# Splitting the weights four units ahead instead of three, with three raw buffers instead of four, and z, one proj_a pair and some short steps moved

## The chip, the core and the metric

The program runs on one core of one Trainium2 chip. Five engines work side by side, each through its own list of instructions, in the order in which the list was built: PE (TensorE, matmuls and transposes), DVE (VectorE), ACT (ScalarE), POOL (GpSimd) and SP (SyncE). SP does nothing here but issue DMAs, POOL does it too. An engine that meets a semaphore that is not yet set stands still, and all that is behind in its list stands with it.

The metric is the device time of one execution in microseconds (us), from its first to its last instruction with what lies around it.

## What is computed

One layer of a decoder for 256 new tokens and 8 running sequences of one token each, 264 columns in all, model width 2048. Cut to what matters:

```python
h = rmsnorm(x, norm1_g)
q, f_logit, i_in, og, u_in, gate_a, gate_b = split(h @ w_in)        # w_in 2048 x 9216
o_h, S_new = hgrn2_recurrence(q, 1 - f, i_in, log(f), S0)           # 8 heads of 128, chunks of 16
o_a = rmsnorm_per_head(o_h) * silu(og)
y5, h_re, h_im = s5_scan(u_in, ...)                                 # 64 groups, 64 complex states each
z = gelu(y5)
zg = z @ w_s5_glu                                                   # 1024 x 2048
o_b = zg[:, :1024] * sigmoid(zg[:, 1024:])
merged = sigmoid(gate_a) * (o_a @ w_proj_a) + sigmoid(gate_b) * (o_b @ w_proj_b)
x = x + merged @ w_out
up = rmsnorm(x, norm2_g) @ w_ffn_up
x = x + (silu(up[:, :5632]) * up[:, 5632:]) @ w_ffn_down
y = rmsnorm(x, final_norm_g)
```

The outputs are y for all tokens and the new recurrent states.

## The kernel before

**Each product is made of three.** Every number is split into a high half that a matmul of the fast fp32r form takes exactly, and the rest: hi = round(w), lo = w - hi. A product is then hi·hi + lo·hi + hi·lo, three matmuls of 128 x 128 weights against 264 columns. The activations (h, oa, z, ob, m, x2g, ff) are split once when they are made, by `X.split`. The weights are split on the way: a **unit** of weights is four chunks of 128 rows by 256 columns, 512 KB; SP loads it into a `raw` buffer, ACT copies it to `hi` (line 151), DVE subtracts to `lo` (line 124). PE then runs 24 matmuls on a unit (4 chunks x 2 column halves x 3). I count the units from 0 in the order of use and write hi(n), lo(n) and L(n) for the high half, the low half and the load of unit n. Units 0 to 3 have two chunks and 12 matmuls.

**The buffers.** `NRAW = 4` raw buffers and `NSPL = 3` pairs of halves. In `gemm` each unit i first calls `load_to(i + NRAW + NSPL - 1)` and `split_to(i + NSPL)`: hi and lo of unit i + 2 are put into the lists of ACT and DVE just ahead of PE's unit i, into the halves that unit i - 1 has just left. L(n) goes into the raw buffer of unit n - 4 and waits on SP until lo(n - 4) has read it.

**The order.** The lists are written out by hand: `gemm` emits the matmuls of a half unit and then calls `advance`, which lets side tasks (generators: `s5_task`, `front_task`, `back_task`, `sample_task`, `z_task`, and evacuations of finished accumulators) put their next instructions behind them. A small model of the clocks of the engines (`clk`, `run`) decides how many steps a task may make; `yield 1` waits until the modelled results are there, `yield 0` only offers a pause. `run_until` forces steps until a condition holds. Nothing of this runs on the chip; what is on the chip is the resulting order.

**The stages.** Start: x is loaded and transposed, its norm is made, and `first_pairs` runs the first two column blocks (u0, u1; units 0 to 9) while `h_task` still makes h, chunk by chunk: DVE t = x·rs (`scaled`), ACT h_hi, DVE h_lo. Its loop gives the two units of a chunk group each a share of the next group's chunks, and `split_to(i + 2)` stands between them. Then the other blocks of w_in that feed HGRN2, S5 and gate b (`TURN`), with the recurrences as side tasks; their small matmuls and transposes stand between the large ones on PE. Then gate a and proj_a in turns (`pa_pair`, p = 0 to 7); `s5_task` ends about here (y of eight tiles, nt = 0 to 7, in place in `u_de`). `z_task` waits until all eight are there ("y") and makes z tile by tile: two GELU, z_hi, z_lo. Then the GLU product on z (four pairs, `glu_evac` makes ob), proj_b on ob (`pb_evac` makes m), w_out on m (`out_evac`), and the feed-forward part in two halves. The norm behind w_out is one matmul on the sum of squares `sqa` (`norm2_evac`).

The transposition of `pn` (parameters of S5), line 164 on PE, opens `s5_task`; DVE copies the last of it (`pn <- ld`, line 139) right before. gn holds the gains of the norms; `lb_evac` transposes it as the first evacuation behind the first pairs.

Of the kernel before, what the change touches and what calls it, by code (L numbers as in the profile page):

```python
# [9 lines left out]
F32 = mybir.dt.float32  # L10
# [20 lines left out]
NRAW = 4  # L31
NSPL = 3
# [33 lines left out]
def hybrid_step(ctx: ExitStack, tc: tile.TileContext, x_prompt, x_sample, state_hgrn, state_s5_re,  # L66
# [159 lines left out]
    for p in range(8):  # L226
        wlist(win, KD, [5120 + UN * q for q in ((0, 1) if p == 0 else (p + 1,) if p < 7 else ())])
        wlist(w_proj_a[0], 8, [UN * p])
    for q in range(4):
        wlist(w_s5_glu[0], 8, [1024 + UN * q, UN * q])  # L230
# [264 lines left out]
    gn = const.tile([64, P], F32, name="gn")  # L495
# [24 lines left out]
    load_to(4)  # L520
# [42 lines left out]
    tp(pg[:, 0, 0:16], gn1, ident[:16, :16])  # L563
    mm(pg[:, 0, 64:65], tok, ss[:, 5:6], True, True)
# [6 lines left out]
    vcopy(gvec[:, 0:16], pg[:, 0, 0:16])  # L571
    ts(vv[:, 2:3], pg[:, 0, 64:65], 1.0 / D, EPS, MUL, ADD)
# [16 lines left out]
    def h_task():  # L589
        t = {}  # L590

        def scaled(c):
            t[c] = spt.tile([P, NT], F32, tag="t", name="t")
            tt(t[c], xt[:, c], rsb if c else pg[:, 1, 0:NT], MUL)

        scaled(0)
        split_to(1)
        act(rsb, pg[:, 1, 0:NT])
        for c in range(KD):
            u = halves(t.pop(c))  # L600
            hi, lo = lying(h.hi[:, c]), lying(h.lo[:, c])
            act(hi, u, scale=gvec[:, c:c + 1])
            if c + 1 < KD:
                scaled(c + 1)
            stt(lo, u, gvec[:, c:c + 1], hi.bitcast(F32), MUL, SUB)
            h.upto(c + 1, clk["v"])
            if c in (2, 4):
                leave(c + 10, px[c // 2 + 1], act)
            yield
# [9 lines left out]
    def lb_evac():  # L619
        yield 1  # L620
        pg, = banks(1)
        tp(pg.t[:, :64], gn, ident[:64, :64])
        yield 1
        vcopy(gvec[:, 16:80], pg.t[:, :64])
        pg.done()
# [124 lines left out]
    def s5_task():  # L750
# [266 lines left out]
        u_done.add("y")  # L1017
# [12 lines left out]
        fo = small([32, 2, P], "fo")  # L1030
        fo2 = h0n
        act(flat(fo), po.t[0:32, 0:256])
# [21 lines left out]
    cmask = hp1.tile([P, 2, P], F32, name="cmask")  # L1054
    G.memset(cmask, 1.0)
    G.affine_select(out=cmask, in_=cmask, compare_op=ALU.is_ge, fill=0.0, base=0, pattern=[[0, 2], [1, P]],
                    channel_multiplier=-1)
    for a in range(2):
        cj = cmask[:, a].rearrange("p (j t) -> p j t", t=16)
        G.affine_select(out=cj, in_=cj, compare_op=ALU.is_ge, fill=0.0, base=0, pattern=[[-16, 8], [0, 16]],  # L1060
                        channel_multiplier=1)
# [75 lines left out]
    def front_task(p):  # L1137
# [98 lines left out]
        for j in range(2):  # L1236
            sv = flat(sc[:, 2 * j:2 * j + 2])
            act(sv, pas[j].t[:, 0:2 * P])
            yield 1
            where(sv, flat(cmask).bitcast(I32), pas[j].t[:, 2 * P:4 * P])  # L1240
            pas[j].done()
# [125 lines left out]
    def gb_evac(p):  # L1367
        def f(acc):
            sg = hp2.tile([P, 2, NT], F32, tag="sgb", name="sgb")
            act(sg, acc, AF.Sigmoid)  # L1370
            gdma(sgb_d[p], sg)
        return f
# [49 lines left out]
    def z_task():  # L1422
        while "y" not in u_done:
            yield 1
        for n in range(8):
            zt = mg2.tile([P, NT], F32, tag="zt", name="zt")
# [9 lines left out]
    for p in range(8):  # L1436
        pa_pair(p)
# [21 lines left out]
    for p in range(4):  # L1459
        sg = mg2.tile([P, 2, NT], F32, tag="sga", name="sga")  # L1460
        gemm(z, 8, sig_evac(sg))
        gemm(z, 8, glu_evac(p, sg))
    mgd = X(xa.tile([P, KD, NT], F32R, tag="xh", name="m_hi"), xa.tile([P, KD, NT], F32R, tag="xl", name="m_lo"))

    def pb_evac(p, sg):
        def f(acc):
            tt(sg, acc, sg, MUL)
            yield 1
# [51 lines left out]
    def norm2_evac():  # L1520
        yield 2
# [147 lines left out]
```

## Time and profile before

| | us |
|---|---|
| three runs before | 1465.81, 1466.18, 1466.27 (median 1466.18) |
| the profiled execution, whole | 1465.0 |
| its span, first to last instruction | 1463.3 |
| PE busy in the span | 1435.1 (98%) |
| DVE busy | 946.5 (65%) |
| ACT busy | 782.4 (53%) |

The matmuls of PE are pipelined: one of 264 columns is shown with 0.28 us, and the next begins 0.11 us after it. So "busy" says only that something was in the pipe, and an idle time that is shown begins when the modelled end of the last one is over. The views that name a wait give idle time only. DVE and ACT are shown with the times of their instructions, which overlap the next by a tenth of a microsecond.

### The profile page before, as it was taken

How to read it: one execution, taken by the hardware profiler on the slowest of the kernel's cores; microseconds unless marked ns; L12 is line 12 of the kernel's file. 1: busy time of each engine (PE TensorE's matmuls, PEld its weight loads, DVE VectorE, ACT ScalarE, POOL GpSimd, SP SyncE). 2: the span in 40 equal slices, each digit the busy share in tenths (PEclk: the TensorE clock that was granted, in tenths of full speed). 3: DMA queues.
4: the chain of work that ended last, by engine and by line, in shares of the span. 5: the costliest groups of instructions: out<-in, count | busy, mean ns of one | idle time of the engine just before them, and what ended most of it. 6: DMA issues, size and time to landing. Idle time of an engine off the chain costs nothing.

```text
span 1463.3 us, 31638 instructions
## 1 busy us (share of the span) xinstructions
PE 1435.1 (98%) x13298; PEld 1417.0 (97%) x13298; DVE 946.5 (65%) x1438; ACT 782.4 (53%) x1109; POOL 94.1 (6%) x170
## 2 busy tenths in 40 slices
PE   8999999999999999999999999999999999999996
PEld 7999999999999999999999999999999999999996
DVE  6588877777688875676665555554545555565553
ACT  6646667676756565445554444443434444445553
POOL 2401010112111010000000000000000000000000
PEclk9999999999999999999999999999999999999998
DMA  7867666677555447666656666655566666665553
GB/s 252 242 197 245 201 200 216 196 215 249 184 156 168 160 146 246 202 220 193 197 188 192 200 191 200 191 191 196 194 202 194 198 193 200 192 199 189 183 188 109
DMA packets 269072, 288.07 MB, mean 197 GB/s; under 512 B 10473, under 2 KB 260729, under 8 KB 268921
## 3 DMA queue, kind: packets, MB, share of 16 engines
q1 hardware_dynamic: 260144, 262.31, 56.2%
q0 software_dynamic: 8512, 23.63, 5.4%
q8 instruction: 104, 1.70, 0.5%
q14 instruction: 40, 0.32, 0.1%
q10 hardware_dynamic: 272, 0.11, 0.0%
HBM read 273.29 MB, written 12.71 MB: 195 GB/s over the span
## 4 chain that ended last, share of the span: by engine, by line
PE 55%; issue 2%; DVE 1%; DMA 0%; ACT 0%; POOL 0%; DVEq 0%; POOLq 0%
PE acc L380 18%; PE acc L379 18%; PE acc L378 18%; PE ps L164 0%; DMA sga<-sgb_d 0%; DVE lo L124 0%; PE ps L159 0%; POOL sga L168 0%; DVE rst L463 0%; DVE sga L124 0%; DVE yns L133 0%; DVE ynp L133 0%; ACT hi L151 0%; DVE rt L124 0%; DVE m_lo L124 0%
## 5 line engine op out<-in xcount | busy, mean ns | idle before, releaser
L124 DVE TENSOR_TENSOR lo<-raw,hi 128x1024 fp32r<-128x1024 f32 (+1 forms) x498 | 596.9, 1202 | 467.1 <-ACT hi L151 461.1
L151 ACT ACTIVATE hi<-raw 128x1024 fp32r<-128x1024 f32 (+1 forms) x498 | 514.8, 1038 | 585.7 <-PE acc L379 514.5
L378 PE MATMUL acc<-x2g_hi,hi 128*128 128x264 f32 x1408 | 388.8, 276 | 0.0
L380 PE MATMUL acc<-x2g_hi,lo 128*128 128x264 f32 x1408 | 388.7, 276 | 0.1
L379 PE MATMUL acc<-x2g_lo,hi 128*128 128x264 f32 x1408 | 388.6, 276 | 0.0
L378 PE MATMUL acc<-h_hi,hi 128*128 128x264 f32 x1088 | 305.7, 281 | 0.7 <-ACT hi L151 0.6
L380 PE MATMUL acc<-h_hi,lo 128*128 128x264 f32 x1088 | 301.3, 277 | 4.0 <-DVE lo L124 4.0
L379 PE MATMUL acc<-h_lo,hi 128*128 128x264 f32 x1088 | 300.3, 276 | 0.0
L380 PEld LDWEIGHTS acc<-x2g_hi,lo 128*128 128x128 f32 x1408 | 266.1, 189 | 0.3 <-DVE lo L124 0.3
L378 PEld LDWEIGHTS acc<-x2g_hi,hi 128*128 128x128 f32 x1408 | 266.1, 189 | 0.0
L379 PEld LDWEIGHTS acc<-x2g_lo,hi 128*128 128x128 f32 x1408 | 266.1, 189 | 0.0
L380 PEld LDWEIGHTS acc<-h_hi,lo 128*128 128x128 f32 x1088 | 205.6, 189 | 5.6 <-DVE lo L124 5.4
L378 PEld LDWEIGHTS acc<-h_hi,hi 128*128 128x128 f32 x1088 | 205.6, 189 | 2.9 <-ACT hi L151 1.1
L379 PEld LDWEIGHTS acc<-h_lo,hi 128*128 128x128 f32 x1088 | 205.7, 189 | 0.2
L378 PE MATMUL acc<-ff_hi,hi 128*128 128x264 f32 x704 | 195.0, 277 | 0.5 <-DVE x L124 0.5
L379 PE MATMUL acc<-ff_lo,hi 128*128 128x264 f32 x704 | 194.3, 276 | 0.0
L380 PE MATMUL acc<-ff_hi,lo 128*128 128x264 f32 x704 | 194.3, 276 | 0.0
L378 PEld LDWEIGHTS acc<-ff_hi,hi 128*128 128x128 f32 x704 | 133.1, 189 | 0.9 <-DVE x L124 0.7
L379 PEld LDWEIGHTS acc<-ff_lo,hi 128*128 128x128 f32 x704 | 133.1, 189 | 0.0
L380 PEld LDWEIGHTS acc<-ff_hi,lo 128*128 128x128 f32 x704 | 133.1, 189 | 0.0
L380 PE MATMUL acc<-m_hi,lo 128*128 128x264 f32 x256 | 70.8, 276 | 0.8 <-DVE lo L124 0.8
L378 PE MATMUL acc<-m_hi,hi 128*128 128x264 f32 x256 | 70.8, 276 | 0.1
(383 smaller groups left out, 1844.4 us busy)
## 6 DMA issues: line engine op xcount, KB each, us to landing
raw<-in_w_ffn_up_dram SPq DMA_DIRECT2D x176, 512.0 KB, 4.6
raw<-in_w_in_dram SPq DMA_DIRECT2D x142, 512.0 KB, 4.6
raw<-in_w_ffn_down_dram SPq DMA_DIRECT2D x80, 512.0 KB, 4.5
raw<-in_w_out_dram SPq DMA_DIRECT2D x32, 512.0 KB, 4.6
raw<-in_w_proj_a_dram SPq DMA_DIRECT2D x16, 512.0 KB, 3.4
raw<-in_w_s_glu_dram SPq DMA_DIRECT2D x16, 512.0 KB, 4.6
raw<-in_w_proj_b_dram SPq DMA_DIRECT2D x16, 512.0 KB, 4.5
s<-in_state_hgrn_dram POOLq DMA_DIRECT2D x8, 512.0 KB, 7.1
```

The costliest lines, as they stand in the source:

```text
L124: V.tensor_tensor(out, a, b, op=op)
L151: S.activation(out, a, f, **kw)
L378: PE.matmul(o, hi[:, q, s], xhi, start=(k0 + q == 0), stop=False)
L379: PE.matmul(o, hi[:, q, s], xlo, start=False, stop=False)
L380: PE.matmul(o, lo[:, q, s], xhi, start=False, stop=(k0 + q == k - 1))
```

## The change

- `NRAW` 3 instead of 4, `NSPL` 4 instead of 3. In `gemm`, hi and lo of unit i + 3 now stand where those of unit i + 2 stood; loads run as far ahead of PE as before (i + 6), through three raw buffers. At the start three loads instead of four are asked for.
- Room for the added halves: gn lies in a pool that ends with the start and is transposed there, with an ACT copy; `cmask` is kept once and broadcast; the S5 output tile `fo` uses `cx`; `sgb` has one buffer instead of two.
- `h_task` multiplies two chunks in one DVE instruction (`scaled`).
- `z_task` starts when tile 5 of S5 is there and takes tiles 6 and 7 as they come.
- The last proj_a pair runs behind the GLU product instead of ahead of it, and its weights are loaded in that order.
- `pb_evac` has one pause less; the matmul of `norm2_evac` is held until the model says that `sqa` is made.

```diff
-NRAW = 4
-NSPL = 3
+NRAW = 3
+NSPL = 4
...
     for p in range(8):
         wlist(win, KD, [5120 + UN * q for q in ((0, 1) if p == 0 else (p + 1,) if p < 7 else ())])
+        if p == 7:
+            for q in range(4):
+                wlist(w_s5_glu[0], 8, [1024 + UN * q, UN * q])
         wlist(w_proj_a[0], 8, [UN * p])
-    for q in range(4):
-        wlist(w_s5_glu[0], 8, [1024 + UN * q, UN * q])
...
-    gn = const.tile([64, P], F32, name="gn")
+    gn = sp.tile([64, P], F32, name="gn")
...
-    load_to(4)
+    load_to(NRAW)
...
     tp(pg[:, 0, 0:16], gn1, ident[:16, :16])
+    tp(pg[:, 0, 128:192], gn, ident[:64, :64])
...
     vcopy(gvec[:, 0:16], pg[:, 0, 0:16])
+    act(gvec[:, 16:80], pg[:, 0, 128:192])
...
         def scaled(c):
-            t[c] = spt.tile([P, NT], F32, tag="t", name="t")
-            tt(t[c], xt[:, c], rsb if c else pg[:, 1, 0:NT], MUL)
+            t[c] = spt.tile([P, 2, NT], F32, tag="t", name="t")
+            if c:
+                e = min(c % 2 + 1, KD - c)
+                tt(t[c][:, 0:e], xt[:, c:c + e], bc(rsb, 1, e), MUL)
+            else:
+                tt(t[0][:, 0], xt[:, 0], pg[:, 1, 0:NT], MUL)
...
-            if c + 1 < KD:
+            if c + 1 < KD and c % 2 == 0:
                 scaled(c + 1)
...
     def lb_evac():
-        yield 1
-        pg, = banks(1)
-        tp(pg.t[:, :64], gn, ident[:64, :64])
-        yield 1
-        vcopy(gvec[:, 16:80], pg.t[:, :64])
-        pg.done()
...
-        u_done.add("y")
+            u_done.add(("y", nt))
...
-        fo = small([32, 2, P], "fo")
+        fo = cx[0:32].rearrange("p r g n -> p r (g n)")
...
-    cmask = hp1.tile([P, 2, P], F32, name="cmask")
+    cmask = hp1.tile([P, P], F32, name="cmask")
...
-            sg = hp2.tile([P, 2, NT], F32, tag="sgb", name="sgb")
+            sg = hp1.tile([P, 2, NT], F32, tag="sgb", name="sgb")
...
     def z_task():
-        while "y" not in u_done:
-            yield 1
         for n in range(8):
+            while ("y", n if n > 5 else 5) not in u_done:
+                yield 1
...
-    for p in range(8):
+    for p in range(7):
         pa_pair(p)
     run_until(lambda: "s5" in u_done)
...
         gemm(z, 8, glu_evac(p, sg))
+    pa_pair(7)
...
             tt(sg, acc, sg, MUL)
-            yield 1
             tt(sg, sg, part[:, 2 * p:2 * p + 2], ADD)
...
     def norm2_evac():
-        yield 2
+        while not at_hand(sqa):
+            yield 1
```

Three places in the lists show what moves. The first is DVE at the end of the first pairs, before: `t` and `h_lo` make two chunks of h, `lo` is the low half of a unit's weights.

```order
L124 TENSOR_TENSOR lo<-raw,hi 128x1024
L124 TENSOR_TENSOR t<-xt,rsb 128x264
L128 SCALAR_TENSOR_TENSOR h_lo<-t,gvec,h_hi 128x264
L124 TENSOR_TENSOR t<-xt,rsb 128x264
L128 SCALAR_TENSOR_TENSOR h_lo<-t,gvec,h_hi 128x264
L124 TENSOR_TENSOR lo<-raw,hi 128x1024
```

And the same place after:

```order
L124 TENSOR_TENSOR lo<-raw,hi 128x1024
L124 TENSOR_TENSOR t<-xt,rsb 128x528
L128 SCALAR_TENSOR_TENSOR h_lo<-t,gvec,h_hi 128x264 x2
L124 TENSOR_TENSOR lo<-raw,hi 128x1024
L124 TENSOR_TENSOR t<-xt,rsb 128x264
L128 SCALAR_TENSOR_TENSOR h_lo<-t,gvec,h_hi 128x264 x2
```

Two products of 264 columns have become one of 528, which stands first behind the `lo`; only the last chunk still has its own.

The second place is DVE behind the first pairs, around the copy `pn`, for which PE's transposition waits. Before, from lo(11) on:

```order
L124 TENSOR_TENSOR lo<-raw,hi 128x1024 x2
L139 COPY gvec<-ps_712 128x64
L124 TENSOR_TENSOR lt<-gvec 128x8
L124 TENSOR_TENSOR lt<-gvec,lt 128x8 x2
L124 TENSOR_TENSOR lo<-raw,hi 128x1024 x2
L124 TENSOR_TENSOR lt<-lt 128x8
L633 RECIPROCAL lt<-lt 128x8
L124 TENSOR_TENSOR lbt<-lt 128x8
L135 TENSOR_SCALAR omlb<-lbt 128x8
L139 COPY pn<-ld_143 32x128
```

After, again from lo(11) on:

```order
L124 TENSOR_TENSOR lo<-raw,hi 128x1024 x3
L124 TENSOR_TENSOR lt<-gvec 128x8
L124 TENSOR_TENSOR lt<-gvec,lt 128x8 x2
L124 TENSOR_TENSOR lo<-raw,hi 128x1024 x2
L124 TENSOR_TENSOR lt<-lt 128x8
L634 RECIPROCAL lt<-lt 128x8
L124 TENSOR_TENSOR lbt<-lt 128x8
L135 TENSOR_SCALAR omlb<-lbt 128x8
L124 TENSOR_TENSOR lo<-raw,hi 128x1024
L139 COPY pn<-ld_143 32x128
```

`pn` stood behind lo(14) and now stands behind lo(16). On PE its transposition moves from the end of unit 12 (264 large matmuls behind the start) to the middle of unit 13 (276).

The third place is ACT at the end of S5: the last states (`hp`, `h`), two output copies, and z. Before:

```order
L151 ACTIVATE hp<-H_266 128x4
L151 ACTIVATE h_1118<-H_266 128x8x4
L151 ACTIVATE fo<-ps_7593 32x256
L151 ACTIVATE h0n<-ps_7594 128x512
L151 ACT_TABLE_LOAD
L151 ACTIVATE zt<-u_de 128x4x64
L151 ACTIVATE zt<-u_de 128x8
L151 ACTIVATE z_hi<-zt 128x264
L151 ACTIVATE hi<-raw 128x1024
L151 ACTIVATE zt<-u_de 128x4x64
L151 ACTIVATE zt<-u_de 128x8
L151 ACTIVATE z_hi<-zt 128x264
```

After:

```order
L151 ACTIVATE hp<-H_266 128x4
L151 ACTIVATE h_1159<-H_266 128x8x4
L151 ACTIVATE cx<-ps_7646 32x256
L151 ACTIVATE h0n<-ps_7647 128x512
L151 ACT_TABLE_LOAD
L151 ACTIVATE zt<-u_de 128x4x64
L151 ACTIVATE zt<-u_de 128x8
L151 ACTIVATE z_hi<-zt 128x264
L151 ACTIVATE hi<-raw 128x1024 x3
L151 ACT_TABLE_LOAD
L151 ACTIVATE sga<-acc 128x528
```

Before, these are the first of eight z tiles; after, seven have been made further up, between S5's own instructions and with table loads of their own (45 on ACT in all, 40 before), and this is the last one. On PE the GLU product now follows the transpositions of hp and h at once, where 72 matmuls of proj_a stood between.

## Rows read from the trace of the kernel before

**Rows 1.** The page, busy time of each engine, its share of the span.

```profile
PE 1435.1 (98%) x13298; PEld 1417.0 (97%) x13298; DVE 946.5 (65%) x1438; ACT 782.4 (53%) x1109; POOL 94.1 (6%) x170
```

**Rows 2.** PE's waits, 43 to 400 us: line, releaser, us, times, longest.

```profile
PE acc L380 <- DVE lo L124: 4.0, 6, 1.2
PE ps L164 <- DVE pn L139: 0.9, 1, 0.9
PE acc L378 <- ACT hi L151: 0.6, 1, 0.6
```

**Rows 3.** PE's waits, 540 to 760 us.

```profile
PE acc L378 <- ACT z_hi L151: 1.3, 2, 0.9
PE acc L378 <- ACT ob_hi L151: 0.9, 1, 0.9
PE acc L379 <- DVE ob_lo L124: 0.9, 1, 0.9
PE acc L379 <- DVE z_lo L124: 0.8, 1, 0.8
PE acc L380 <- DVE lo L124: 0.8, 1, 0.8
```

**Rows 4.** PE's instructions around one wait: start, us, operation, idle before, releaser.

```profile
75.07 0.28 PE L379 MATMUL acc<-h_lo,hi 128*128 128x264 f32 x1
76.12 0.38 PE L380 MATMUL acc<-h_hi,lo 128*128 128x264 f32 x1 [0.77 <-DVE lo L124]
76.33 0.28 PE L378 MATMUL acc<-h_hi,hi 128*128 128x264 f32 x1
```

**Rows 5.** Stretches: us, busy (count) of each engine, granted clock, DMA share.

```profile
601.00:604.40 3.40, 3.40 (x18) 3.40 (x18) 0.00 (x0) 1.06 (x1) 0.00 (x0) 0.50 0.48 155
740.00:1340.00 600.00, 599.94 (x5333) 599.74 (x5332) 336.79 (x328) 263.62 (x273) 0.00 (x0) 1.00 0.61 195
```

**Rows 6.** One turn of the first pairs in time, DVE, ACT and PE.

```profile
27.50 0.43 DVE L124 TENSOR_TENSOR t<-xt,rsb 128x264 f32<-128x264 f32 x1
27.96 0.55 ACT L151 ACTIVATE h_hi<-t,gvec 128x264 fp32r<-128x264 f32 x1 [1.20 <-DVE t L124]
28.41 1.04 ACT L151 ACTIVATE hi<-raw 128x1024 fp32r<-128x1024 f32 x1
29.48 1.23 DVE L124 TENSOR_TENSOR lo<-raw,hi 128x1024 fp32r<-128x1024 f32 x1 [0.39 <-ACT hi L151]
30.76 0.49 PE L410 MATMUL acc<-h_hi,lo 128*128 128x264 f32 x2 [0.16 <-DVE lo L124]
```

**Rows 7.** A DVE product of 528 columns from the stage of proj_b.

```profile
642.78 0.71 DVE L124 TENSOR_TENSOR m_lo<-sga,m_hi 128x528 fp32r<-128x528 f32 x1 [0.78 <-ACT m_hi L151]
```

**Rows 8.** Behind the first pairs: DVE, ACT and PE in time.

```profile
41.59 1.23 DVE L124 TENSOR_TENSOR lo<-raw,hi 128x1024 fp32r<-128x1024 f32 x1 [1.48 <-ACT hi L151]
42.94 0.80 ACT L151 ACTIVATE u_de<-acc 128x256 f32<-128x256 f32 x4 [1.39 <-PE acc L410]
52.30 0.30 PE L164 MATMUL ps<-ident,pn 96*128 96x96 f32 x1 [0.87 <-DVE pn L139]
```

**Rows 9.** Loads of raw, from issue to landing: 36 to 62 us; 900 to 1000; 315 to 345.

```profile
DMA to landing us min/median/max: 4.0/5.1/6.6
...
DMA to landing us min/median/max: 2.8/4.5/4.7
...
DMA to landing us min/median/max: 3.5/6.5/9.1
```

**Rows 10.** SP's waits over the whole span, the longest line.

```profile
SPq L246 <- DVE lo L124: 1016.7, 419, 7.0
```

**Rows 11.** ACT and PE at the end of S5.

```profile
539.52 0.36 PE L378 MATMUL acc<-oa_hi,hi 128*128 128x264 f32 x1
540.42 1.28 ACT L151 ACT_TABLE_LOAD   x1
542.43 0.46 ACT L151 ACTIVATE z_hi<-zt 128x264 fp32r<-128x264 f32 x1
```

More of the change, by code (lines that the diff above doesn't have):

```diff
@@ L599, in h_task @@
         for c in range(KD):
-            u = halves(t.pop(c))
+            u = halves(t[c - (c > 0 and c % 2 == 0)][:, int(c > 0 and c % 2 == 0)])
             hi, lo = lying(h.hi[:, c]), lying(h.lo[:, c])
             act(hi, u, scale=gvec[:, c:c + 1])
-            if c + 1 < KD:
+            if c + 1 < KD and c % 2 == 0:
                 scaled(c + 1)
@@ L1029, in s5_task @@
         yield 2
-        fo = small([32, 2, P], "fo")
+        fo = cx[0:32].rearrange("p r g n -> p r (g n)")
         fo2 = h0n
-        act(flat(fo), po.t[0:32, 0:256])
+        act(fo, po.t[0:32, 0:256].rearrange("p (r x) -> p r x", r=2))
         act(fo2.rearrange("p r a x -> p (r a x)"), po2.t)
@@ L1052, in hybrid_step @@
     G.memset(smask.rearrange("p (c t) -> p c t", t=16)[:, :, 0], 0.0)
-    cmask = hp1.tile([P, 2, P], F32, name="cmask")
+    cmask = hp1.tile([P, P], F32, name="cmask")
     G.memset(cmask, 1.0)
-    G.affine_select(out=cmask, in_=cmask, compare_op=ALU.is_ge, fill=0.0, base=0, pattern=[[0, 2], [1, P]],
+    G.affine_select(out=cmask, in_=cmask, compare_op=ALU.is_ge, fill=0.0, base=0, pattern=[[1, P]],
                     channel_multiplier=-1)
[L1058 to L1061, printed above, removed]
+    cj = cmask.rearrange("p (j t) -> p j t", t=16)
+    G.affine_select(out=cj, in_=cj, compare_op=ALU.is_ge, fill=0.0, base=0, pattern=[[-16, 8], [0, 16]],
+                    channel_multiplier=1)
     q2 = hp1.tile([P, 4, 8, 16], F32, name="q2")
@@ L1239, in front_task @@
             yield 1
-            where(sv, flat(cmask).bitcast(I32), pas[j].t[:, 2 * P:4 * P])
+            where(sc[:, 2 * j:2 * j + 2], bc(cmask.bitcast(I32), 1, 2),
+                  pas[j].t[:, 2 * P:4 * P].rearrange("p (m t) -> p m t", m=2))
             pas[j].done()
```

## The prediction

> **What bounds the kernel now.** The page first: PE is busy 98% of the span, DVE 65%, ACT 53% [rows 1], so the time is PE's work plus what PE waits, and the change leaves the number of large matmuls as it is. From 740 to 1340 us PE starts 5333 matmuls in 599.94 us of 600 [rows 5]: 0.1125 us each, 2.70 for the 24 of a unit, nothing to be won there. So PE's waits come next, stage by stage: what there is to win is in the list for 43 to 400 us [rows 2] and that for 540 to 760 [rows 3], about 10 us of idle time together. The timeline around one wait tells what idle time is worth: a matmul should follow its forerunner by 0.11, here 75.07 is followed by 76.12 and that by 76.33, so 0.94 and 0.10 are lost where 0.77 of idle time is shown [rows 4]. **Each wait costs its idle time and 0.27.**
>
> **What the halves give.** hi and lo of unit i + 3 stand where those of i + 2 stood and wait for the same halves, those of unit i - 1. A split takes 1.05 on ACT and 1.23 on DVE, 2.3 with the hand-over [rows 6, 8], so in the steady state lo is done 3 x 2.70 - 2.4 = 5.7 ahead of its use instead of 3.0. The six waits for lo and the one for hi in the stretch from 43 to 400 are DVE or ACT arriving at most 1.2 late behind side work [rows 2]. One unit more, 2.7, covers each of them. Worth 4.0 + 0.6 + 7 x 0.27 = **6.5**; ends 3 and 6.5, since DVE may fall further back when PE no longer waits for it. The same holds for the wait for lo of 0.8 at the start of w_out [rows 3]: **1.1**.
>
> **What the raw buffers take.** SP's loads wait for lo nearly always [rows 10]. With four buffers a load may take 4 x 2.70 - 2.4 = 8.4 us before the next split is late, with three 5.7. In the feed-forward part loads take 4.5 (at most 4.7), from 315 to 345 us 6.5 with a maximum of 9.1 [rows 9]. So the long stages are safe and the bursts are not: a load of 9.1 makes a unit cost (9.1 + 2.3)/3 = 3.8, 1.1 over PE's 2.70, and the lead of 5.7 carries five such units. ACT and DVE stand behind a late load, though, with side work in their lists, and PE may meet a transposition that needs it. No row of before shows that; bounds 0 and 3 (one load late by 9.1 - 5.7 = 3.4), I take **-1.5**.
>
> **The joined products.** In the first pairs [rows 6] each turn is a ring: t (27.50), h_hi, which waited for it (idle 1.20), hi (28.41), lo (29.48 + 1.23), the next t; PE waits for that lo at 30.76. 3.1 us a turn against PE's 2.70: the ring sets the pace. In it stands now a product of 528 columns, 0.71 by the nearest row [rows 7], where one of 264 took 0.43 [rows 6]: 0.28 more in each of five turns, 1.4. DVE has fewer instructions, but gains nothing in time, because it idles in the ring (0.39 for hi). L(3) and L(4) also wait for lo(0) and lo(1) now; I add 0.1. **-1.5** at unit 9; ends -1 and -2.5.
> The Trainium skill weighs this both ways: Perfetto Trace Analysis, section Optimizing Scalar/DVE Operations, advises grouping into larger operations when the engine is saturated (it gives some 60 ns of overhead per DVE instruction), and breaking instructions up when an engine that is not saturated causes bubbles elsewhere. By the first half seven instructions less would be an estimated gain of 0.4 in place of the loss, and the sum below 1459.0. The rows speak for the second half.
>
> **The early stall.** No row of before shows this one; it is worked out lap by lap. PE's transposition of pn waits for a DVE copy that stood behind lo(14) and now stands behind lo(16), while PE itself arrives half a unit later than before. PE's own way: unit 9 ended at 42.9 (u_de had waited for it [rows 8]), now 44.4; three and a half units more, 9.45: 53.9. DVE's way: lo(10) ended at 41.59 + 1.23 = 42.8 [rows 8], now 44.3. L(13) waits for it, since there are three buffers. A load takes 5.1 here (4.0 to 6.6) [rows 9]: 49.4; split 2.3: lo(13) at 51.7. L(16) waits for that: 56.8; lo(16) 59.1; pn 0.3 later: 59.4. PE stands for 5.5 us. Before, it did the transposition at 52.30 [rows 8] with twelve matmuls (1.35) less behind it: the loss up to here, the 1.5 of the ring in it, is 59.4 - 52.3 - 1.35 = **-5.8**. With loads of 4.0 it is 3.6, with 6.6 8.8. What a stall does to the clock, the stage of ob shows: two idle times of 0.93 close together [rows 3], then the granted clock is 0.50, the lower of its two levels (1.2 GHz), for 3.4 us [rows 5]; that costs half of 3.4. I take the same here, **-1.7**, ends 0 and 1.7.
> Afterwards units 14 to 16 are split already, and the lead is there.
>
> **z.** Before, eight tiles are made in a row while PE is already at the product: 1.3 + 0.8 idle in three waits [rows 3], 2.9. Now only tile 7 is left. On the old time axis PE enters the GLU product at 539.5, behind the transpositions [rows 11], and meets tile 7 after 33 matmuls, at 543.2; its z_hi ends at 542.43 + 0.46 = 542.9 [rows 11], z_lo 0.43 later, 543.4. **+2.7.** Its cover is thin: 0.2 late already, and a table load (1.28 [rows 11]) more in front would cost that much.
> Seven tiles made among sigmoids bring five more table loads, 6.4 us of ACT at 1.28 [rows 11]; ACT is idle 47% [rows 1], and the splits are 5.7 ahead, so they cost nothing.
> The Trainium skill speaks against it: ScalarE: Activation LUTs, section Rules for kernel authors, says to do all of one table set before switching and to budget about 2.7 us for a switch, an estimated 13.5 here; the trace shows half of that for the load itself. What would follow is the fourth rival.
>
> **ob.** proj_b waits at its second unit for the last pair of ob: 0.9 + 0.9 idle [rows 3], 2.3 with the surcharge, and the half clock behind it [rows 5], 1.7. The last proj_a pair, 48 matmuls or 5.4 us, now stands between; the chain was some 3 late. **+4.0**, the clearest term.
>
> **At nothing.** gn at the start: its transposition stands in PE's list behind those of x, some ten instructions long; up to 0.5 if its DMAs are later than x's. cmask, fo and sgb: same work, in smaller room; sgb's store has the time of a block between two uses. The pause in pb_evac and the hold of norm2_evac: up to 0.5 in favour. Cover for all of these is PE's large matmuls; together bounds -1 and +1.
>
> **The sum.** 6.5 + 1.1 + 2.7 + 4.0 = 14.3 gained; 5.8 + 1.7 + 1.5 = 9.0 lost; 5.3 less. Against the profiled execution, 1465.0, that is 1459.7; the median of the three runs is 1.2 above it, so **1460.9**.
>
> **Rivals.**
> First: the early stall doesn't come or is short, because with fewer loads under way each takes less than 4.0. For it: three loads share the queues, not four; against it: stores of u and of x use them as well, and 4.0 is the least in the stretch [rows 9]. Then only the ring's 1.5 is left of 5.8 and 1.7, and no burst: 1466.2 - 14.3 + 1.5 = 1453.4.
> Second: the waits of 43 to 400 us come back. DVE is the late one in six of seven [rows 2]; if it cannot do its work in less time, PE saves little by being ahead: 3.5 of the 6.5 lost, or bursts at their bound of 3: 1463 to 1466, with both.
> Third, on the other side: bursts. Each of the four head pairs brings its states in and out, and loads of 9.1 then [rows 9]; if the late load blocks the side work that PE meets next, it costs 3.4 each time. All four: 1460.9 - 1.5 + 4 x 3.4 = 1473.0; it is slower than before by over 0.2% from three of four on. Against it: the lead of 5.7 covers PE's weights, and the side steps are placed some slots behind what they need.
> Fourth: the table loads meet the path. If they and the z tiles push the splits or S5's own steps, PE pays the 6.4 and z's gain remains: 1467.3.
> Fifth: the change gives no lead at all. That can't be for the split, whose place in the lists is plain.
>
> **How the numbers follow.** Forecast 0.54, first rival 0.20, second 0.17, third 0.05, fourth 0.04. The range reaches from the first rival to the second's upper end, each with the 1 of the edits at nothing: 1452.4 to 1467. A measurement can tell about 0.2% from no change, 2.9 us: faster is below 1463.3, slower above 1469.1. Faster: 0.54 + 0.20 and some of the second, 0.03, 0.77. Slower: the third, 0.05. Same: 0.18.
>
> **What would show it.** Right: a wait of PE for pn of several us near 54 to 60, with a stretch of clock 0.50 behind; no wait for ob; at most 0.5 for z; in 43 to 400 else no wait for lo; lo done some 5.7 ahead of use in the feed-forward part. The ring right: turns of 3.4 between 25 and 37 us. Wrong: pn waits under 2 us (then loads were quicker, first rival), waits of PE for ps tiles during bursts (third), z waiting over 1 us.

## The result, and the profile after

The changed kernel takes 1489.0 us (median of four runs, 1486.2 to 1491.3), the kernel before 1466.0 in the same comparison: the ratio is 1.016, with a 95% interval from 1.015 to 1.018. Forecast were 1460.9 and a gain, 1452.4 to 1467 as the range; the worst of the rivals, the third, gave 1473.0. The profiled execution, 1490.3 whole, is read here against the one of before.

The page of the changed kernel, busy time and share of the span, to be read against [rows 1]: PE has 4.1 us more of it, and the span is 25.3 longer. The rest, 21.2, is time in which PE is shown idle.

```profile
PE 1439.2 (97%) x13298; PEld 1422.9 (96%) x13298; DVE 948.1 (64%) x1430; ACT 791.7 (53%) x1115; POOL 93.4 (6%) x169
```

PE's waits from 43 to 400 us, as in [rows 2] (line, releaser, us, times, longest):

```profile
PE ps L159 <- DVE qz L139: 10.9, 3, 9.5
PE ps L164 <- DVE pn L139: 6.1, 1, 6.1
PE acc L379 <- DVE sm L139: 2.9, 1, 2.9
PE ps L159 <- ACT ro L151: 1.9, 3, 1.1
PE acc L379 <- ACT hi L151: 1.8, 1, 1.8
PE ps L159 <- ACT Cc L151: 1.8, 1, 1.8
PE ps L159 <- ACT Kb L151: 1.6, 1, 1.6
PE acc L381 <- DVE lo L124: 0.8, 2, 0.6
```

The waits for lo fell from 4.0 to 0.8 us; the forecast had none left. What has come are waits for side steps, nearly all of small matmuls (L159, L164), those for sm and hi of large ones (L379): `qz`, `ro` and `sm` belong to HGRN2, `pn`, `Cc` and `Kb` to S5. Only pn was in the forecast's sum; waits of the third rival's kind had 0.05. PE's waits where [rows 3] stood, 560 to 790 us:

```profile
PE acc L379 <- DVE zo L124: 2.0, 1, 2.0
PE acc L379 <- DVE part L124: 0.6, 1, 0.6
```

The waits for z, ob and w_out's lo are gone; one for `zo` is new. Stretches of the changed kernel (us, busy of the engines, granted clock, DMA share), as in [rows 5]: after a stall the granted clock is 0.50, its lower level, for some us (the first stretch, with 0.62, holds both levels; PE had waited 1.6 for a hi just ahead of it), and the feed-forward part is what it was.

```profile
28.00:32.40 4.40, 4.36 (x24) 4.36 (x25) 3.74 (x6) 2.28 (x4) 0.00 (x0) 0.62 0.39 123
63.00:66.20 3.20, 2.66 (x13) 2.67 (x14) 0.61 (x3) 0.00 (x0) 3.20 (x7) 0.50 0.93 281
334.00:336.00 2.00, 2.00 (x11) 2.00 (x11) 1.77 (x6) 0.68 (x1) 0.00 (x0) 0.50 0.00 0
740.00:1340.00 600.00, 600.00 (x5334) 599.94 (x5333) 340.53 (x338) 267.25 (x277) 0.00 (x0) 1.00 0.62 195
```

**The same matmul in two traces** says best where the time went. All kernels here run the same 11712 large matmuls, so the start of the n-th in one trace can be set against its start in another. The table gives that difference to the kernel before, in us, for each profiled execution (behind 5640 nothing moves any more). It holds two things: time that PE lost, and PE's own small work that one kernel does earlier than the other. Of the second I give an estimate where it matters, from the number of small rows and what each kind takes in the trace of before; from 3960 on all kernels have done the same.

```
n                        0   240   360   720  1800  2040  2160  3120  3600  3960  4320  5640
before, starts at     16.7  48.6  63.7 109.8 250.7 287.6 304.2 443.3 512.2 564.7 609.2 760.6
the change            +2.0  +4.7 +11.3  +9.9 +16.3 +19.0 +38.4 +35.7 +34.3 +31.9 +27.8 +25.4
after_raw4            +0.4  +1.9  +5.3  +3.5  +6.6  +7.8 +28.9 +25.2 +24.5 +19.9 +15.8 +13.4
before_raw3           +0.0  +1.1  +1.8  +2.5  +4.0  +4.5  +4.5  +8.8  +8.8 +10.2 +10.2 +10.0
before_split4         -0.6  +0.1  +6.1  +4.3  +5.1  +5.4  +5.4  +5.4  +5.4 +11.0  +9.3  +7.6
before_raw4_split4    +0.1  +0.1  +2.9  +1.1  -0.3  -0.3  -0.3  -2.5  -2.5  +2.8  +1.1  -0.6
after_side3           +0.0  +2.5  +9.8  +8.1  +7.9  +8.1  +8.1 +14.5 +13.5 +14.8 +10.7  +8.3
after_side3_raw4      +0.1  +1.6  +2.7  +0.8  -0.5  -0.5  -0.5  +1.2  +2.3  +1.2  -2.9  -5.3
best_guess            +0.0  +0.0  -1.1  -1.4  -2.8  -2.8  -2.8  -1.2  -2.2  -4.8  -8.8 -11.2
best_three_ahead      -0.8  -0.8  -1.8  -2.3  -2.3  -2.3  -2.3  -0.7  -1.2  -3.8  -7.8 -10.3
after_pn_early        +0.3  +1.8  +0.7  +3.6 +10.5 +16.7 +37.8 +34.3 +32.9 +32.1 +28.0 +25.6
after_two_ib          -0.0  +1.7  +8.5  +8.3 +16.9 +19.7 +38.8 +40.7 +39.3 +38.5 +34.4 +32.0
before_forced         -1.1  -1.1  -1.1  -1.6  -1.6  -1.6  +8.0 +11.2 +14.2  +4.1  +2.4  +2.5
after_spread          +0.7  +3.4  +9.8  +8.1 +17.6 +19.7 +32.2 +42.0 +40.6 +39.8 +35.8 +33.3
before_plan24         -0.8  -0.8  -0.8  -1.3 +16.2 +10.1 +12.0 +14.6 +14.9  +6.1  +6.1  +5.9
before_plan26         -0.6  -0.6  -0.4  -1.0  -3.6  -2.0  +4.2  +1.2  +4.2  -0.9  -0.9  -1.0
after_plan24          -0.2  +2.3 +10.2  +8.4 +10.6 +18.0 +30.4 +26.3 +25.9 +36.4 +32.4 +29.9
after_plan26          +0.5  +3.4  +9.9  +9.8 +11.3 +15.2 +14.5 +11.7 +13.2 +26.3 +22.2 +19.8
```

Row "the change": 4.7 are lost by the end of the first pairs, 6.6 around pn, 28.5 from 720 to 2160, of which 19.4 in the last 120 matmuls. In these PE has 100 small rows where the kernel before has 28, so some 4.7 of the 19.4 is work that stands earlier (an estimate), and comes back later. From there on the kernel gains, 13.0 in all: what was forecast for ob, w_out and the norm (4.06, 1.4 and 1.05), 0.9 of z, and for the most part of the rest the moved work.

The long stretch in the trace of the changed kernel, PE's small instructions and then DVE (start, us, operation, idle time before). Between large matmuls 2111 and 2112 PE has 18.4 us of this; in the kernel before the longest such gap is 4.3.

```profile
315.77 1.04 PE L164 MATMUL ps<-ident,ext 128*128 128x128 f32 x8
326.35 1.08 PE L159 MATMUL ps<-s,qz 128*32 128x128 f32 x16 [9.54 <-DVE qz L139]
...
316.90 1.21 DVE L124 TENSOR_TENSOR s<-s,ib 128x1024 f32<-128x1024 f32 x1
...
319.38 1.21 DVE L124 TENSOR_TENSOR lo<-raw,hi 128x1024 fp32r<-128x1024 f32 x1
324.07 1.22 DVE L124 TENSOR_TENSOR ib<-ib,sm 128x1024 f32<-128x1024 f32 x1 [3.47 <-DMA ib<-is_d]
...
326.03 0.17 DVE L139 COPY qz<-sm 128x8 f32<-128x8 f32 x1
```

PE is at qz's matmuls at 316.8; in DVE's list s + ib, a split, and a product with ib whose load has not landed stand ahead of the copy.

### The profile page after: what moved, and what is told of

Same layout as the page of the kernel before. It is cut to its first block, busy times and chain, and to the rows that moved or that the text cites. A ratio compares the mean times of both kernels' runs of the same rounds, so it can differ in the third digit from the quotient of the medians.

```text
span 1488.6 us, 31711 instructions
## 1 busy us (share of the span) xinstructions
PE 1439.2 (97%) x13298; PEld 1422.9 (96%) x13298; DVE 948.1 (64%) x1430; ACT 791.7 (53%) x1115; POOL 93.4 (6%) x169
## 4 chain that ended last, share of the span: by engine, by line
PE 79%; DMA 7%; DVE 6%; ACT 6%; issue 2%; POOL 0%; SPq 0%; DVEq 0%; ACTq 0%; POOLq 0%
PE acc L379 25%; PE acc L380 24%; PE acc L381 24%; DMA raw<-in_w_in_dram 5%; PE ps L159 4%; DVE lo L124 3%; ACT hi L151 2%; PE ps L164 1%; ACT s L151 1%; ACT L151 1%; DVE t L124 1%; DMA raw<-in_w_s_glu_dram 1%; DMA x_d<-xt 1%; DMA gn<-in_lb_logits_dram 0%; DMA ib<-is_d 0%
## 5 line engine op out<-in xcount | busy, mean ns | idle before, releaser
L379 PE MATMUL acc<-x2g_hi,hi 128*128 128x264 f32 x1408 | 389.3, 276 | 0.0
L379 PE MATMUL acc<-h_hi,hi 128*128 128x264 f32 x1088 | 308.1, 283 | 4.8 <-DVE sm L139 2.9
L379 PEld LDWEIGHTS acc<-x2g_hi,hi 128*128 128x128 f32 x1408 | 266.5, 189 | 0.0
L379 PEld LDWEIGHTS acc<-h_hi,hi 128*128 128x128 f32 x1088 | 207.8, 191 | 7.0 <-ACT hi L151 3.1
L379 PE MATMUL acc<-ff_hi,hi 128*128 128x264 f32 x704 | 195.2, 277 | 0.5 <-DVE x L124 0.5
L379 PEld LDWEIGHTS acc<-ff_hi,hi 128*128 128x128 f32 x704 | 133.3, 189 | 0.9 <-DVE x L124 0.7
L380 PE MATMUL acc<-m_lo,hi 128*128 128x264 f32 x256 | 70.8, 276 | 0.0
```

Of the source, the lines that this page charges most:

```text
L379: PE.matmul(o, hi[:, q, s], xhi, start=(k0 + q == 0), stop=False)
L380: PE.matmul(o, hi[:, q, s], xlo, start=False, stop=False)
```

## The experiments

Two suspects could be told apart, because the order of the side steps comes from the planner and not from the chip: the planner can be told of one number of buffers while the kernel has another. **Theory buffers**: three raw buffers make the splits on ACT and DVE stand for their loads, with side steps behind. **Theory order**: the lists planned anew put side steps where their inputs come late, whatever the buffers.

**1. after_raw4**: the change with four raw buffers, all lists unchanged.

```diff
-NRAW = 3
+NRAW = 4
+MODEL = {"raw": 3}
...
+            tag, bufs = own.get(n, (tag, MODEL.get(str(tag).split("_")[0], bufs)))
```

> The changed kernel with four raw buffers instead of three and nothing moved: every engine's list stands in the order of the changed kernel (the planner is told of three). Room is made by letting sgb, isn and ro use the room of sg, o2 and fw, and z's two scratch tiles have one buffer each. Theory buffers (three raw buffers make the splits on ACT and DVE stand for their loads, the side steps stand behind them, and PE meets side steps that are not ready): ACT's waits for raw from 40 to 450 us fall from 54.6 to under 15, the wait for pn (6.1) and its half clock (1.7) go, of the waits for qz, sm, Cc, Kb, ro in 200 to 400 us (17.3 and about 5 of half clock) under 4 is left: about 1458, between 1453 and 1464. Theory order (the splits put one unit earlier into the lists make the planner place side steps where their inputs come late, whatever the buffers): only pn and its clock, 8, go: about 1481, between 1477 and 1485.

1479.1 (ratio 1.0096, 1.0081 to 1.0111): 9.9 less than the change, within the range of theory order and 21 above the value of theory buffers. But ACT's waits for raw from 40 to 450 us, the mark of theory buffers, did what it said; before, the change, and this kernel:

```profile
ACT hi L151 <- DMA raw<-in_w_in_dram: 5.0, 3, 2.0
```

```profile
ACT hi L151 <- DMA raw<-in_w_in_dram: 54.6, 31, 5.4
```

```profile
ACT hi L154 <- DMA raw<-in_w_in_dram: 4.8, 3, 2.7
```

The 54.6 went back to 4.8, and yet the stretch from 2040 to 2160 still costs 21.1, and PE's longest wait, from 43 to 450 us, is the old one:

```profile
PE ps L162 <- DVE qz L142: 10.1, 1, 10.1
PE ps L167 <- DVE pn L142: 2.7, 1, 2.7
```

Each theory holds for a part.

**2. before_raw3**: the other way round, the kernel before with three raw buffers, all lists unchanged (`NRAW = 3`, `MODEL = {"raw": 4}`, loads still asked for at unit i + 6).

> The kernel before with three raw buffers instead of four and nothing moved: every list as before, halves three units ahead. Theory buffers: ACT waits for raw for 40 us or more from 40 to 450 us (5.0 before), PE waits for lo and for side steps: 1480 to 1495. Theory order: the lists are those of before, so only single late loads show, 1466 to 1472.

1475.7 (1.0076, 1.0059 to 1.0093): 11.3 lost, below what theory buffers gave and above the other. ACT stands for raw again, 40 to 450 us:

```profile
ACT hi L154 <- DMA raw<-in_w_in_dram: 52.0, 27, 6.9
```

In the table the loss comes in small steps, with 4.3 between 2160 and 3120.

**3. before_split4** and **4. before_raw4_split4**: halves four ahead, with three and with four raw buffers, side steps in the order of before. The splits go into the lists early, and the planner hears of them a unit later:

```diff
-            act(hi[:, :k], t[:, :k])
-            tt(lo[:, :k], t[:, :k], hi[:, :k].bitcast(F32), SUB)
+            S.activation(hi[:, :k], t[:, :k], AF.Copy)
+            V.tensor_tensor(lo[:, :k], t[:, :k], hi[:, :k].bitcast(F32), op=SUB)
+            unseen.append((t, hi, lo, k))
...
-            split_to(i + NSPL)
+            split_to(i + NSPL, i + 3)
```

> The kernel before with halves four units ahead in three raw buffers, as the change has it, but the side steps on all engines in the order of before: on ACT and DVE only the splits stand one unit earlier, PE's list is that of before. Room as in the change (cmask, fo) and by sgb in the room of sg and single scratch tiles for z. Theory buffers: the raw buffers cost here what they cost in the changed kernel, less what the first pairs' joined products cost: 1476 to 1490. Theory order: the lead gains its 7.6, the copy of pn stands behind one split more and costs up to 5: 1459 to 1466.

> As the one before it, with four raw buffers: halves four ahead, no raw buffer given up, side steps in the order of before. Isn and ro use the room of o2 and fw, Cc that of pn. Both theories: the lead without its price, by the sum of the prediction 6.5 + 1.1 = 7.6 less than before, 1458.5, between 1456 and 1462; lo is done about 5.7 us ahead of its use in the feed-forward part, and PE's waits for lo from 43 to 400 us (4.0 before) go. If the time stays at 1464 or more, the waits for lo were not worth what the sum says.

1474.2 (1.0062, 1.0047 to 1.0077) and 1464.6 (1.0004, 0.9994 to 1.0014). The first lies between the theories, the second above its range. Between the two it is the raw buffers (and small changes of room) that differ: 9.6. Neither has the 20 near 2160. The second gains nothing that can be measured with the lead alone: its row shows 5.4 gained from 360 to 3120, 2.8 lost ahead of that at pn (the copy stands behind one split more, PE waits 2.0) and 5.3 lost at z. The last, I infer, and no run shows it alone, is the price of the single scratch tile that made room: PE waits four times for z_hi, 2.2 us, where before it was twice.

**5. after_side3** and **6. after_side3_raw4**: the change, with the side steps planned as if the splits stood three ahead, and with three or four raw buffers.

> The changed kernel, its three raw buffers and four halves kept, with the side steps planned as if the splits stood three units ahead; only the splits themselves stand four ahead in the lists of ACT and DVE. Two forced rounds at unit 90, none at the end of S5 (the planner lets S5 run 4.0 us ahead instead of 2.5 behind the last head pair, for otherwise 15 forced rounds stand there). Theory forced row: the 22 us that large matmuls 1800 to 2160 lost go and the raw buffers' 10 stay: 1467, between 1463 and 1472. Theory buffers alone: they also make these waits: 1480 or more.

> As the one before it, every list in the same order, with four raw buffers (room as in the first run with four). If the two causes add: 1489 less 22 less 10 = 1457, between 1453 and 1461, faster than the kernel before by what the late moves (ob 4.1, w_out 1.4, norm2 1.0, z 3) and the lead give, less the start's 2 and the wait for pn (3). If one cause contains the other: 1463 or more.

1473.7 (1.0072, 1.0050 to 1.0093) and 1461.4 (0.9975, 0.9965 to 0.9985). The first missed its value by 7 and its range by 1.7, the second by 4 and 0.4. The order is worth 15.3 with three buffers and 17.7 with four, the fourth buffer 12.3 here and 9.9 in the order of the change: the two causes add within some 2.4. With both gone the change beats the kernel before, by 0.25%. (The better order differs from the change's in one more number, how far S5 may run ahead at its end; behind the last head pair 15 rounds would be forced without it.)

**7. before_forced**: is it the row of small instructions? At unit 90 the planner had forced five rounds of side steps (two before), and 38 small PE instructions stand in a row between two large ones (15 before; in the trace, where each matmul of L159 has two rows, 66 and 28).

```diff
             run_until(lambda: "e" in d)
+            if p == 3:
+                st["hurry"] = True
+                for _ in range(3):
+                    advance(True)
+                st["hurry"] = False
```

> The kernel before with one thing added: when the q product of the last head pair is evacuated (unit 90), the side tasks are forced for three more rounds, so five as in the changed kernel, where before has two. PE's list gets 35 small instructions in a row there, between two large matmuls, where 15 stood (38 in the changed kernel). Buffers as before. Theory forced row: PE meets a chain that DVE, ACT and a DMA have not finished, with nothing large to do meanwhile; in the changed kernel this stretch (large matmuls 2040 to 2160) cost 19.4, with four raw buffers 21.1: here 10 to 20 more, 1474 to 1485, with waits of PE for qz or its like of over 5 near 300 us. Theory late engines (the row is harmless where ACT and DVE are on time): under 1468.

1468.9 (1.0029, 1.0019 to 1.0040): 4.2, under the range of the forced row and just above the other's. The stretch itself costs 9.6, some 2.3 of it moved work, and the longest wait in it is 4.3, for o on ACT, where one of over 5 was the mark of the row. Most is given back later (from +14.2 at 3600 to +2.4): S5 was driven ahead here, and from 3600 to 3960, where the kernel before has 188 small rows, this one has none.

**8. after_two_ib** takes away the late load, with a second buffer for ib; **9. after_spread** takes away the row, by forcing one round behind each half of units 87 to 89.

```diff
+        ibs = []
+        for j in range(2):
+            t = hp1.tile([P, NS, P], F32, tag=f"ib{j}", name="ib")
...
+            G.dma_start(t, is_d[p, :, j * P:j * P + P].partition_broadcast(P))
+            ibs.append(t)
```

> The changed kernel with two buffers for ib instead of one, so that the second load of ib is issued right behind the first and no longer waits on POOL until s + ib has read the one buffer; all else in the order of the changed kernel (room by sgb in sg, isn in o2, ro in fw, Cc in pn). In the trace of the changed kernel DVE stood 3.5 us for that load with qz behind it, and PE stood 9.5 for qz. If the late load is a part of the long wait: DVE's wait for it goes, PE's wait for qz falls to 5 to 6.5, the whole from 1489 to 1485, between 1483 and 1487. If the load is all of it: 1478 to 1481. If it is none (the chain behind it ends no earlier): 1488 or more.

> The changed kernel with one forced round of the side tasks behind each half of units 87, 88 and 89, so that little is left to force at unit 90: one round there instead of five, and the 38 small PE instructions in a row become rows of 2, 8 and 12 with large matmuls between. Buffers and all that stands before unit 87 are as in the changed kernel; behind unit 90 the planner goes on from another state (three rounds are forced where the last head pair ends). Theory row: it is the standing of PE's small instructions in one row, with no large matmul to do, that costs 19.4 between large matmuls 2040 and 2160; spread, that stretch costs under 8, and the whole falls by 7 to 15, to 1474 to 1482. Theory late DVE: DVE's and ACT's lists hold more work ahead of these steps than PE's does, wherever they stand: PE waits about as long in other places, and the whole stays at 1486 or more.

1491.3 (1.0175, 1.0158 to 1.0192) and 1496.5 (1.0210, 1.0192 to 1.0229): neither is a gain. With two buffers DVE no longer waits for ib, but ACT and PE come to the same place as late, because ACT now stands for raw (ACT, DVE and PE in the trace of after_two_ib):

```profile
315.06 1.06 ACT L154 ACTIVATE hi<-raw 128x1024 fp32r<-128x1024 f32 x1 [2.41 <-DMA raw<-in_w_in_dram]
...
323.69 1.22 DVE L127 TENSOR_TENSOR ib<-ib,sm 128x1024 f32<-128x1024 f32 x1
...
325.96 1.08 PE L162 MATMUL ps<-s,qz 128*32 128x128 f32 x16 [5.77 <-DVE qz L142]
```

Spread, PE waits for qz in the very gap between 2111 and 2112, which now holds 24 rows in place of 66:

```profile
327.75 1.08 PE L159 MATMUL ps<-s,qz 128*32 128x128 f32 x16 [9.27 <-DVE qz L139]
```

That stretch costs 12.5 instead of 19.4, where under 8 was the mark of the row, another gap of 10.7 comes behind 2687, and the whole is 7.5 slower. So it is neither the row nor that load alone: in this order DVE's and ACT's lists hold some 10 us more ahead of these steps than PE's does, as the waits of 9.5, 10.1 and 9.3 say, and taking away one wait shows the next.

**10. after_pn_early** moves one DVE instruction, the copy of pn, right behind the first pairs.

> The changed kernel with DVE's copy of pn right behind the first pairs, behind lo(11) instead of lo(16); no other instruction moves on any engine. This is the term 'early stall' of the prediction by itself (there 4.3 beyond the ring and 1.7 of half clock, 6.0). If it was right: no wait for pn (6.1), no half clock from 60 to 66 us, the time falls by 5 to 7, to about 1483. If the late raw buffers only move the wait to the next step on PE: it falls by under 3, to 1486 or more.

1488.5 (1.0160, 1.0135 to 1.0184; its four runs lie between 1485.0 and 1493.4): 0.5 less than the change, where 5 to 7 would have shown that the stall is a cost by itself. The wait for pn is gone (+0.7 at 360 against +11.3), and by 1800 the kernel is late by 10.5 again, by 2160 by 37.8. The order of PE's list is the same in both, so I read it thus: PE had only waited early for engines that were late anyway.

**11. best_guess** puts together what had held, and **12. best_three_ahead** is the same with three pairs of halves.

```diff
 NRAW = 4
-NSPL = 3
+NSPL = 4
...
+    for t in tasks:
+        t.ahead = LATE_S5
...
     first_pairs(h, (u_evac(0), u_evac(1)))
+    vcopy(pn[64:96].rearrange("t (g n) -> t g n", g=2), bc(ld2[64:96], 2, 64))
```

> The kernel before with four raw buffers and four halves, the side steps planned as for three halves, single products t, gn as before, the copy of pn put right behind the first pairs, and of the change the early z, the last proj_a pair behind the GLU, the joined step of proj_b and the hold of the norm's matmul; S5 runs 4.0 ahead at its end. By what the runs measured: 1464.4 - 5.6 (waits of the h stage) - 1.4 (w_out) - 4.1 (ob) - 3 (z) - 1 (norm) = 1449, between 1446 and 1455. If the lead makes the engines that feed side steps later, or table loads meet the path at the end of S5: 1456 or more.

> The best kernel so far (1453.5) with three pairs of halves instead of four: on ACT and DVE the splits stand one unit later, every other instruction on every engine where it was. It measures the lead alone. By the prediction's terms 6.5 + 1.1 = 7.6 more, 1461; by the runs with the lead so far, 5.6 + 1.4 = 7.0 more, 1460.5, between 1459 and 1462, and PE waits for lo again, 4 us or so in all from 43 to 400 us. If the lead is worth less because DVE and ACT are late with side steps instead: 1457 or less.

1453.5 (0.9926, 0.9911 to 0.9942), the fastest here, 0.7% under the kernel before, within its range and 4.5 above its value; and 1455.5 (0.9933, 0.9918 to 0.9948), which can't be told from it. The forecast for the lead, 7, failed; the other branch, 1457 or less, held. PE's waits from 43 to 400 us show why; three ahead, then four:

```profile
PE acc L393 <- DVE lo L265: 3.2, 5, 1.2
PE ps L163 <- ACT CA L155: 1.9, 1, 1.9
PE ps L163 <- ACT o L155: 0.5, 1, 0.5
```

```profile
PE ps L163 <- ACT CA L155: 2.3, 1, 2.3
PE ps L168 <- DVE k L128: 1.6, 2, 1.4
PE acc L391 <- ACT hi L264: 1.1, 1, 1.1
PE ps L163 <- ACT o L155: 0.5, 1, 0.5
```

The 3.2 for lo go, and 3.1 come back for side steps and hi: 5.6 idle before, 5.5 after. DVE and ACT do the same work in another order, and PE meets what now stands last.

**13 to 16. before_plan24, before_plan26, after_plan24, after_plan26**: is the cost of the order the change's own? One number of the planner, by how much side tasks may run ahead of PE, is 2.4 or 2.6 instead of 2.5 us (`AHEAD`, `AHEAD_S5`).

> The kernel before with one number of the planner changed: side tasks may run 2.4 us ahead of PE in its model instead of 2.5. Buffers, splits and work as before; some 250 rows of PE's list and 120 of DVE's stand in another order. Theory any new order: the former order was tuned, a new one costs much of what the changed kernel's did: large matmul 3120 starts 8 to 20 later than in the kernel before, the whole 1473 to 1486. Theory the change's own: a replanned list without the splits further ahead costs little: large matmul 3120 within 4 of before, the whole under 1470.

> The same with 2.6 us. Theory any new order: 1473 to 1486, large matmul 3120 later by 8 to 20. Theory the change's own: under 1470, within 4.

> The changed kernel with 2.4 us instead of 2.5. Its large matmul 3120 starts 35.7 later than before's. Theory any new order: the orders differ among each other, this one between 15 and 40. Theory the change's own: every order planned with these splits and buffers loses about the same, 30 to 40. Behind the last head pair 20 rounds are forced at the end of S5 where the changed kernel has none; what they cost shows behind large matmul 3600 and is left out of the comparison.

> The changed kernel with 2.6 us instead of 2.5; two rounds forced at unit 90 instead of five, 21 at the end of S5. Large matmul 3120: theory any new order, between 10 and 40 later than before's; theory the change's own, 30 to 40.

1471.3 (1.0043, 1.0027 to 1.0058), 1463.4 (0.9988, 0.9978 to 0.9998), 1493.3 (1.0198, 1.0178 to 1.0218) and 1484.8 (1.0140, 1.0107 to 1.0174). At large matmul 3120 the kernel before is late by 14.6 or by 1.2 with a new order, the changed one by 26.3 or 11.7, where it was 35.7. Moved work is in these: before_plan24 has 112 small rows more behind it there than the kernel before, after_plan26 86 fewer. Without it, by the estimate above, it is some 10 and 0 for the kernel before, 28 and 15 for the changed one, which was at 33. In before_plan24 it is qz again:

```profile
PE ps L159 <- DVE qz L139: 5.6, 1, 5.6
PE acc L380 <- DVE lo L124: 4.5, 6, 1.2
```

Neither theory holds as it was put: a new order may cost next to nothing, or 10 up to there in the kernel before (6.5 in its whole time), and more in the changed one. Of three orders the change has drawn the worst up to 3120; the 15 of after_plan26 is little more than the three buffers alone cost (at 3120 the sixth run has 13.3 less than the fifth). The whole times of the last two can't be set against the change's, because 20 and 21 rounds are forced at the end of S5, with a gap of 17.4 and 19.6 between 3791 and 3792. That three buffers make bad orders worse can't be excluded by these four.

## Why the prediction was wrong

**The order of the side steps had no term.** The prediction showed three places of the lists and priced those; that hundreds of side instructions had been placed anew from 40 to 500 us was priced at nothing. It was 15.3 to 17.7 us, the largest item. (Between forecast and result lie 28.1: this, 2.1 to 4.8 by which the raw buffers cost more than was said, and 5.6 by which the lead gave less, 23.0 to 28.1 together.) The third rival saw PE wait for side steps, with the bursts as cause, 3.4 each and a chance of 0.05; against it stood that "the side steps are placed some slots behind what they need". That premise failed: the planner places them by modelled times, and the trace has qz 9.5 us late.

**What the raw buffers take** was put at 1.5 (0 to 3), with 6.0 more around pn (5.8 less the ring's 1.5, and the clock's 1.7): 7.5. It is 9.6 to 12.3 in four pairs of kernels. Right was that PE's weights are covered (0.8 of waits for lo) and that the feed-forward part is safe (nothing moves behind 5640). The step that failed is the one that I had named and then bounded too low: "ACT and DVE stand behind a late load, though, with side work in their lists". The new wait at the GLU shows it in small, ACT and DVE of the changed kernel:

```profile
590.68 1.06 ACT L151 ACTIVATE hi<-raw 128x1024 fp32r<-128x1024 f32 x1 [4.44 <-DMA raw<-in_w_s_glu_dram]
...
591.77 1.23 DVE L124 TENSOR_TENSOR lo<-raw,hi 128x1024 fp32r<-128x1024 f32 x1 [4.27 <-ACT hi L151]
592.91 0.70 DVE L124 TENSOR_TENSOR zo<-acc,sga 128x528 f32<-128x528 f32 x1
```

PE needs no weight here; it needs the accumulator that zo empties, and zo stands behind a split that stands for its load. With four raw buffers (after_raw4, after_side3_raw4) there is no wait for zo.

**The early stall** came, by the way that was worked out: ACT stands for the loads ahead of the copy, and PE waits 6.1 for pn where 5.5 was said, then with a clock of 0.50 for some 3 us:

```profile
58.59 1.06 ACT L151 ACTIVATE hi<-raw 128x1024 fp32r<-128x1024 f32 x1 [2.34 <-DMA raw<-in_w_in_dram]
60.92 1.06 ACT L151 ACTIVATE hi<-raw 128x1024 fp32r<-128x1024 f32 x1 [1.27 <-DMA raw<-in_w_in_dram]
...
63.54 0.42 PE L164 MATMUL ps<-ident,pn 96*128 96x96 f32 x1 [6.08 <-DVE pn L139]
```

That 5.5 came so near is in part luck: PE was there at 57.5 instead of 53.9, and the copy ended at 63.5 instead of 59.4, both about 4 later. As a term of the sum it was wrong: moving the copy gave 0.5, for the time was lost on DVE and ACT, not at that wait.

**What the halves give**: 6.5 and 1.1 forecast. The lead itself came: from 760 to 950 us lo is done 5.87 ahead of its use (median), 3.17 in the kernel before, and from 100 to 400 us 5.0, where it was 2.1. What failed is its worth. In the lists of before (before_raw4_split4) the h stage gained 5.4 and lost 2.8 at pn; with nothing but the splits moved (the two best kernels) the whole gain is 2.0 between medians that can't be told apart, 1.0 between their traces. This is the second rival's reason ("if it cannot do its work in less time, PE saves little by being ahead"), and it took more than the 3.5 of 6.5 that the rival gave it. w_out's 1.4 comes with the lead and the old pb_evac (before_raw4_split4) and without the lead with the new one (best_three_ahead); either is enough.

**The joined products**: 1.5 forecast, 1.5 measured from 0 to 240 with four raw buffers (after_raw4, after_side3_raw4; best_guess, with single products, has 0.0). With three it is 1.5 to 2.9 in seven kernels, and the change's own 2.7 has the half clock between 28 and 32.4 us in it, which five of these seven show and none with four: the 0.1 for later loads was too small. The turn is 3.4, lo to lo, as forecast:

```profile
33.55 1.23 DVE L124 TENSOR_TENSOR lo<-raw,hi 128x1024 fp32r<-128x1024 f32 x1 [0.45 <-ACT hi L151]
34.70 0.70 DVE L124 TENSOR_TENSOR t<-xt,rsb 128x528 f32<-128x528 f32 x1
...
36.96 1.23 DVE L124 TENSOR_TENSOR lo<-raw,hi 128x1024 fp32r<-128x1024 f32 x1 [0.44 <-ACT hi L151]
```

By the second half of the advice in the Trainium skill (Perfetto Trace Analysis, section Optimizing Scalar/DVE Operations), to break instructions up where an engine that is not saturated causes bubbles elsewhere, this was to be expected, and the trace agrees.

**ob, z, norm**: ob gave 4.06 of 4.0 in every kernel that has the move. z gave 3.2 with four raw buffers (2.7 forecast, no wait for z left), 0.9 in the change, where zo's wait, 2.0 idle, took the rest. The hold of the norm's matmul gave 1.05, twice its bound. The Trainium skill (ScalarE: Activation LUTs, section Rules for kernel authors) counsels against the five more table loads. They take 1.28 each here. In the change itself, in after_raw4 and in the two best kernels no wait of PE for z or behind a table load shows from 400 us on, so the fourth rival is not what happened. In after_side3_raw4 it shows in small: z tiles and a load stand ahead of sga on ACT, and PE waits 1.8 for it, then 1.3 for ext:

```profile
499.15 1.28 ACT L155 ACT_TABLE_LOAD   x1
500.44 0.61 ACT L155 ACTIVATE sga<-acc 128x528 f32<-128x528 f32 x1
...
501.10 0.38 PE L391 MATMUL acc<-h_hi,hi 128*128 128x264 f32 x1 [1.77 <-ACT sga L155]
```

**Open** is which of the displaced side steps make the 15 to 18: the late load, the row and the copy of pn each fell as sole cause. Open is also whether this order costs so much by itself or because halves stand four ahead on ACT and DVE: no run has the change's order of side steps with halves three ahead.

## What to carry to other kernels

Where an order is planned by modelled times, an edit that looks local re-deals the whole order: read both lists for steps that an in-order engine meets long before its partner, and test the edit with the old order kept, or its own worth can't be seen (here some 16 us of order hid the 10 that the moves behind it gained: 4.06, 1.4, 1.05 and z's 3.2). A buffer taken from the loads costs the engines that stand in front of it, and what else they have in their lists, even where the consumer never waits for that data. A wait on the busiest engine is worth what is left once the next late thing stands there: two waits that were removed here, 6.1 and 3.2 us, gave back 0.5 and 2.

## What the runs showed of the hardware

Eight kernels with the same start (gn transposed there) begin their large matmuls between 0.2 us earlier and 0.7 later than the kernel before, but for the changed kernel's own execution, 2.0 later with a granted clock of 0.57 from 8 to 16 us, where the eight have 1.00. So a start of 16 us can vary by 2 between executions of one order, and one trace does not price an edit there.
